# An encoder layer on one core: its attention stage with three engines in a hand-set order

## The chip, the cores and the metric

The kernel runs on one core of one Trainium2 chip. The metric is the device time of one execution, in microseconds (us); the times of three executions of the kernel before are given below. All rows come from one profiled execution. The engines are TensorE (PE, the matrix products; PEld is its weight loading), DVE (VectorE), ACT (ScalarE), POOL (GpSimd) and SP, whose queue issues the DMAs.

## The reference, cut to what matters

One layer with three branches: latent attention with 8 heads over 1024 positions, a short convolution, and cross-attention to 256 memory rows, each with a gate, mixed and projected. All in float32. The change concerns this part:

```
def blocked_bidirectional_attention(q, k, v):      # q, k: 8 heads of 96; v: 8 heads of 64
    def one_block(q_blk):                          # 128 query rows
        s = jnp.einsum('bqhd,bkhd->bhqk', q_blk, k).astype(jnp.float32) * scale
        p = jax.nn.softmax(s, axis=-1).astype(v.dtype)
        return jnp.einsum('bhqk,bkhd->bqhd', p, v)
...
o_attn = blocked_bidirectional_attention(q, k, v) * jax.nn.silu(g_attn)
...
r_attn, r_conv, r_mem = split_cols(jax.nn.sigmoid(r + b_gate), (D_MODEL, D_MODEL, D_MODEL))
y = r_attn * (o_attn @ w_br_attn) + r_conv * (o_conv @ w_br_conv) + r_mem * (o_mem @ w_br_mem)
return x + y @ w_out
```

## The kernel before, in words

A float32 product is made of three products of rounded parts: a value is split into a high half (a rounded copy) and a low half (value minus high half), and high by high, high by low and low by high are added in PSUM. The helper `split` does this with two instructions, the first at L74 (POOL) or L76 (ACT), the second at L80.

The attention stage is the function `mla`. It runs over 64 blocks i of 128 query rows (8 heads, 8 blocks each); two blocks make a pair u. For a block, `sm(i)` makes the scores (six products, L931, into one of two PSUM buffers `s`), the negated row maximum on DVE (L933), the exponential with its row sum on ACT (L936), the reciprocal of the sum (L937), and then turns the block: a float32 cannot be turned by the DMA, so DVE copies its two 16-bit planes into `pl` (`planes`, L85) and two DMA transposes on the SP queue bring them to `plt` (L86). `t(i)` puts the words together again with two ACT copies into `pw` (`words`, L90), then makes the high half `pth` on POOL (L74) and the low half `ptl` on DVE (L80). `pv(u)` needs the halves of both blocks: two small products that spread the reciprocals (L960), eight products with `pth` (L962), eight with `ptl` (L964). It ends with a copy `otmp` on ACT (L971), two additions and scalings on DVE (L972, L973) and, for every second head, a gate and a split on POOL and two stores.

Into this stage the generator `dense` weaves the projection of x that the mixing gates need ("filler products" here, L519, L521 and L523 into `mm`): `pull(n)` takes n of them. 48 belong to one weight tile (an item), whose split on POOL is one pair of instructions of 1024 columns; each 24 are taken out of PSUM by ACT (L613). After the last block come the filler products that are left, then the branch products (L705, L707, L709) with the tiles `oc`, `om` and `oa`.

TensorE's instructions run in the order in which the program writes them (`manual_schedule` from the memory attention on). The order of DVE, ACT, POOL and SP is set by a planner with a cost estimate. Each engine works off its own list in turn, and waits where an operand is not there. In iteration i the program writes: `sm(i)`, 3/8 of the filler products of the iteration, `pv((i-7)/2)` at every second i, `t(i-3)`, the other filler products; 96 filler products are kept for behind the loop.

Of the kernel before, what the change touches and what calls it, by code (L numbers as in the profile page):

```python
# [9 lines left out]
F32 = mybir.dt.float32  # L10
F32R = mybir.dt.float32r
# [3 lines left out]
ALU = mybir.AluOpType  # L15
# [3 lines left out]
P = 128  # L19
S = 1024  # L20
D = 1024
TB = S // P
# [8 lines left out]
NB = 256  # L31
# [30 lines left out]

class K:
# [161 lines left out]
    def phase1(self, sr):  # L225
        tc, nc, a, d = self.tc, self.nc, self.a, self.d
        v, gp = nc.vector, nc.gpsimd
        with ExitStack() as st:
            wk = self.pool(st, "wk0")
# [181 lines left out]
            raws = [load_w(0)]  # L411
# [13 lines left out]
            for t in range(2, TB):  # L425
# [17 lines left out]
                if t >= 3 and up:  # L443
                    src, h_, l_, k = up.pop(0)
                    n = src.shape[-1]
# [7 lines left out]
            ps = self.ps = self.psum(st, "ps00")  # L453
# [1 line left out]
            self.items[0].update(eng="AP")  # L455
            self.gen = self.dense(self.items)
            next(self.gen)
            self.pulled = 0
            self.mm = lambda hf: ps.tile([P, 512], F32, name="fm", bufs=3)
            wd = self.pool(st, "wk1")  # L460
            self.pl = {n: wd.tile([P, 2, H, P], U16, name="pl" + n) for n in "kq"}
# [16 lines left out]
    def dense(self, items):  # L478

        nc = self.nc  # L480
        raws, ws = {}, {}

        def load(i):
            if i < len(items) and i not in raws:
                raws[i] = items[i].get("raw") or self.wp.tile([P, 1024], F32, name="wraw", bufs=2)
                nc.sync.dma_start(raws[i], items[i]["src"])

        def split(i):
            if i < len(items):
                dst = items[i].get("dst")  # L490
                if dst is None:
                    dst = [self.wp.tile([P, 1024], F32R, name=n, bufs=2) for n in ("whi", "wlo")]
                load(i)
                self.split(raws[i], dst[0], dst[1], *items[i].get("eng", "P"))
                ws[i] = dst

        load(0)
        split(0)
        yield
        load(1)  # L500
        i = -1
        while i + 1 < len(items):
            i += 1
            split(i + 1)
            load(i + 2)
            wh, wl = ws.pop(i)
            if "body" in items[i]:
                yield from items[i]["body"](wh, wl)

    def feat(self, fin):  # L510

# [397 lines left out]
    def mla(self, st, sh):  # L909
        tc, nc, a, d = self.tc, self.nc, self.a, self.d  # L910
        v, ps = nc.vector, self.ps
        nj = NB // P
        NBLK = S // NB
        self.o = {}
        wk_s = st.enter_context(ExitStack())
        wk = self.pool(wk_s, "wk5", side="right")
        HD, load = self.HD, self.load_head
        PL, PT, MX, cur = {}, {}, {}, {}

        def sm(i):  # L920
            h, tb = divmod(i, TB)
            k = HD[h][0]
            if i % nj == 0:
                self.load_q(i // nj + 2)
            q = self.QB[i // nj]
            ts = slice(i % nj * P, (i % nj + 1) * P)
            s = ps.tile([P, S], F32, name="s", bufs=2)
            for qi, ki, s_, e_ in ((0, 0, True, False), (0, 1, False, False), (1, 0, False, True)):
                for hf in range(2):
                    c = slice(hf * 512, hf * 512 + 512)  # L930
                    nc.tensor.matmul(s[:, c], q[:, qi, ts], k[:, ki, c], start=s_, stop=e_)  # L931
            mx = MX[i] = wk.tile([P, 4], F32, name="mx", bufs=10)
            v.reduce_max(out=mx[:, 1:2], in_=s, axis=AX.X, negate=True)  # L933
            p = wk.tile([P, S], F32, name="p", bufs=2)

            nc.scalar.activation(out=p, in_=s, func=AF.Exp, bias=mx[:, 1:2], accum_out=mx[:, 2:3])  # L936
            v.reciprocal(mx[:, 3:4], mx[:, 2:3])  # L937
            PL[i] = wk.tile([P, 2, TB, P], U16, name="plt", bufs=3)
            self.planes(p, wk.tile([P, 2, S], U16, name="pl", bufs=2), PL[i])

        def t(i):
            u, j = divmod(i, nj)
            js = slice(j * P, (j + 1) * P)
            if j == 0:
                PT[u] = [wk.tile([P, TB, NB], F32R, name="pt" + x, bufs=2) for x in "hl"]
            p = wk.tile([P, TB, P], F32, name="pw", bufs=2)
            self.words(p, PL.pop(i))
            self.split(p, PT[u][0][:, :, js], PT[u][1][:, :, js], "P", "V")

        def pv(u):  # L950
            h, blk = divmod(u, NBLK)
            bs = slice(blk * NB, (blk + 1) * NB)
            vv = HD[h][1]
            pth, ptl = PT.pop(u)

            pb = ps.tile([P, 2, NB], F32, name="po", bufs=2)
            po, rb = pb[:, 0], pb[:, 1]
            for j in range(nj):
                r = MX.pop(u * nj + j)[:, 3:4]
                nc.tensor.transpose(rb[:, j * P:(j + 1) * P], r.broadcast_to([P, P]), self.ident)  # L960
            for kb in range(TB):
                nc.tensor.matmul(po, vv[:, kb, :], pth[:, kb, :], start=kb == 0, stop=False)  # L962
            for kb in range(TB):
                nc.tensor.matmul(po, vv[:, kb, :], ptl[:, kb, :], start=False, stop=kb == TB - 1)  # L964
            pr, od = divmod(h, 2)
            if od == 0 and blk == 0:
                cur["o"] = wk.tile([P, S], F32, name="o", bufs=1)
            o = cur["o"]
            a0, b0 = (0, 64) if od == 0 else (64, 0)
            tmp = wk.tile([P, NB], F32, name="otmp")  # L970
            nc.scalar.copy(tmp[a0:a0 + 64, :], po[b0:b0 + 64, :])  # L971
            v.tensor_tensor(out=o[a0:a0 + 64, bs], in0=po[a0:a0 + 64, :], in1=tmp[a0:a0 + 64, :], op=ALU.add)  # L972
            v.tensor_tensor(out=o[a0:a0 + 64, bs], in0=rb[a0:a0 + 64, :], in1=o[a0:a0 + 64, bs], op=ALU.mult)  # L973
            if od == 1:
                gp = nc.gpsimd
                oh = wk.tile([P, NB], F32R, name="oah")
                ol = wk.tile([P, NB], F32R, name="oal")
                ga = wk.tile([P, NB], F32, name="ga")
                nc.sync.dma_start(ga, d["ga"][:, pr, bs])
                gp.tensor_tensor(out=o[:, bs], in0=o[:, bs], in1=ga, op=ALU.mult)  # L980
                self.split(o[:, bs], oh, ol)
                nc.sync.dma_start(d["oah"][:, pr, bs], oh.bitcast(F32))
                nc.sync.dma_start(d["oal"][:, pr, bs], ol.bitcast(F32))

        N = H * TB
        r_end = 1248 + 24 * 48
        rest = 96
        for i in range(N + 7):
            if i % TB == TB - 4 and 0 < i // TB < H:
                load(i // TB + 1)  # L990
            n = (r_end - rest - self.pulled) // (N + 7 - i)
            if i < N:
                sm(i)
                self.pull(n * 3 // 8)
            if i == 0:
                with tc.issue_after(self.turned):
                    load(1)
            if i >= 7 and (i - 7) % 2 == 0:
                pv((i - 7) // 2)
            if 0 <= i - 3 < N:  # L1000
                t(i - 3)
            self.pull(n - n * 3 // 8 if i < N else n)
        wk_s.close()
        self.alloc_o(self.pool(self.st, "oc", side="right"), "oc")
        step(self.load_o("oc"))
        self.ahead(2)
        self.pull_to(r_end)
        self.s_kvq.close()
        sh.close()
        self.open_out()  # L1010
# [134 lines left out]
```

## Time and profile before

| | us |
|---|---|
| median of three executions | 1223.88 |
| lowest, highest | 1223.3, 1226.05 |
| the profiled execution | 1220.76 |
| its span, first to last instruction | 1219.0 |
| busy in the span: TensorE, weight loading | 1146.2, 961.0 |
| busy: DVE, ACT, POOL | 709.7, 546.4, 501.9 |
| mean granted clock of TensorE | 0.975 |
| first to last score maximum of the attention stage | 591.1 to 949.4 |

The span is read by stretches, since the stages have different limits. Busy time of TensorE counts a product that runs at half clock as twice the time, so it does not say what is left to gain; the granted clock beside it does (1.00 is 2.4 GHz, 0.50 is 1.2 GHz). A row of the timeline gives start, duration, engine and line of an instruction, and in brackets how long the engine was idle before it and what ended that.

### The profile page before, as it was taken

The numbers are of one execution on the slowest core, as the hardware profiler recorded it, in microseconds if no ns is written. First come the engines' busy times: TensorE is split into PE (matmuls) and PEld (weight loads), VectorE is DVE, ScalarE is ACT, GpSimd is POOL, SyncE is SP. The second block draws the span as 40 slices with busy tenths as digits, with TensorE's granted clock in tenths as the row PEclk, the third lists the DMA queues.
The fourth block names the chain that finished last, engine by engine and source line by source line (L and its number), as shares of the span: only waits on it lengthen the run. The fifth ranks groups of instructions, "written<-read, shape, count | busy, mean of one in ns | idle before, by whom it ended". The sixth has DMA issues, their size and how long they took to land.

```text
span 1219.0 us, 15240 instructions
## 1 busy us (share of the span) xinstructions
PE 1146.2 (94%) x5458; PEld 961.0 (79%) x5458; DVE 709.7 (58%) x1084; ACT 546.4 (45%) x821; POOL 501.9 (41%) x382
## 2 busy tenths in 40 slices
PE   8999998999999999899988979889798999999998
PEld 7998786788888887777766768677687878888887
DVE  6997785253335345553478887878888503655221
ACT  6445766311112035554487676757767522323100
POOL 4456455332325633345334543433554533323200
PEclk8999998999999999999999899998999999999999
DMA  8428999823324243548697896887876589545341
GB/s 304 149 78 203 226 252 233 234 72 104 104 89 136 88 108 100 127 134 223 179 198 179 172 237 168 190 189 162 204 185 147 166 310 387 152 147 171 123 138 52
DMA packets 283821, 207.75 MB, mean 170 GB/s; under 512 B 201440, under 2 KB 253280, under 8 KB 282976
## 3 DMA queue, kind: packets, MB, share of 16 engines
q1 hardware_dynamic: 283744, 206.76, 62.7%
q8 instruction: 43, 0.70, 0.3%
q14 instruction: 34, 0.28, 0.1%
HBM read 108.14 MB, written 50.33 MB: 130 GB/s over the span
## 4 chain that ended last, share of the span: by engine, by line
PE 45%; ACT 14%; DMA 14%; DVE 13%; issue 9%; POOL 4%; SPq 1%; ACTq 0%; DVEq 0%; POOLq 0%
DMA plt<-pl 9%; ACT pw L90 7%; PE mm L519 6%; PE mm L523 6%; PE mm L521 6%; DVE pl L85 5%; PE mm L707 4%; PE mm L705 4%; PE mm L709 4%; ACT p L936 3%; DVE ptl L80 3%; PE mm L109 3%; PE mm L110 3%; PE mm L111 3%; PE pq L293 2%
## 5 line engine op out<-in xcount | busy, mean ns | idle before, releaser
L519 PE MATMUL mm<-hh,whi 128*128 128x512 f32 x672 | 268.9, 400 | 3.4 <-DVE sg L596 2.5
L523 PE MATMUL mm<-hh,wlo 128*128 128x512 f32 x672 | 267.1, 399 | 1.2 <-POOL wlo L80 1.2
L521 PE MATMUL mm<-hl,whi 128*128 128x512 f32 x672 | 267.9, 399 | 0.0
L90 ACT COPY pw<-plt 128x1024 uint16<-128x1024 uint16 (+1 forms) x160 | 201.3, 1300 | 133.7 <-DMA plt<-pl 85.4
L74 POOL TENSOR_SCALAR whi<-wraw 128x1024 fp32r<-128x1024 f32 x59 | 70.5, 1195 | 226.3 <-PE mm L521 78.0
L519 PEld LDWEIGHTS mm<-hh,whi 128*128 128x128 f32 x672 | 130.3, 194 | 31.7 <-DVE sg L596 3.4
L80 POOL TENSOR_TENSOR wlo<-wraw,whi 128x1024 fp32r<-128x1024 f32 x60 | 152.1, 2535 | 5.4 <-ACT whi L76 1.6
L523 PEld LDWEIGHTS mm<-hh,wlo 128*128 128x128 f32 x672 | 130.2, 194 | 29.3 <-POOL wlo L80 1.6
L521 PEld LDWEIGHTS mm<-hl,whi 128*128 128x128 f32 x672 | 130.1, 194 | 27.1
L931 PE MATMUL s<-k,q 96*128 96x512 f32 x384 | 107.4, 417 | 41.3 <-ACT p L936 40.6
L74 POOL TENSOR_SCALAR pth<-pw 128x1024 fp32r<-128x1024 f32 x64 | 82.9, 1299 | 134.8 <-ACT pw L90 115.1
L85 DVE COPY pl<-p 128x1024 uint16<-128x1024 uint16 x144 | 128.8, 936 | 7.8 <-POOL p L830 6.0
L931 PEld LDWEIGHTS s<-k,q 96*128 96x128 f32 x384 | 73.6, 197 | 66.7 <-ACT p L936 50.2
L80 DVE TENSOR_TENSOR ptl<-pw,pth 128x1024 fp32r<-128x1024 f32 x64 | 88.3, 1381 | 5.9 <-POOL pth L74 5.5
L933 DVE TENSOR_REDUCE mx<-s 128x1 f32<-128x1024 f32 x64 | 77.1, 1215 | 6.0 <-PE s L931 5.4
L936 ACT ACTIVATE p<-s,mx 128x1024 f32<-128x1024 f32 x64 | 71.0, 1111 | 12.4 <-DVE mx L933 9.7
L682 ACT ACTIVATE sg<-sg 128x1024 f32<-128x1024 f32 x24 | 25.4, 1062 | 85.9 <-DMA sg<-d_r 81.3
L391 ACT COPY pw<-plt 96x512 uint16<-96x512 uint16 x64 | 43.8, 772 | 27.3 <-DMA plt<-plq 18.6
L613 ACT ACTIVATE sg<-mm,small 128x512 f32<-128x512 f32 x48 | 32.9, 687 | 42.0 <-PE mm L523 37.0
L937 DVE RECIPROCAL mx<-mx 128x1 f32<-128x1 f32 x64 | 10.3, 161 | 60.8 <-ACT p L936 60.6
L712 DVE TENSOR_TENSOR acc<-mm,sg 128x512 f32<-128x512 f32 x16 | 10.8, 688 | 57.0 <-PE mm L709 43.6
L76 ACT CAST whi<-wraw 128x1024 fp32r<-128x1024 f32 x9 | 9.5, 1052 | 68.4 <-PE mm L521 66.8
(322 smaller groups left out, 2359.1 us busy)
## 6 DMA issues: line engine op xcount, KB each, us to landing
wraw<-in_w_feat SPq DMA_DIRECT2D x48, 512.0 KB, 4.3
d_r<-sg SPq DMA_DIRECT2D x24, 512.0 KB, 3.1
sg<-d_r SPq DMA_DIRECT2D x24, 512.0 KB, 3.8
d_k<-qkt SPq DMA_DIRECT2D x32, 192.0 KB, 3.1
d_q<-qkt SPq DMA_DIRECT2D x32, 192.0 KB, 3.1
q<-d_q SPq DMA_DIRECT2D x32, 192.0 KB, 3.3
k<-d_k SPq DMA_DIRECT2D x8, 768.0 KB, 7.3
wraw<-in_w_br SPq DMA_DIRECT2D x12, 512.0 KB, 4.4
```

What stands on the lines that cost most here:

```text
L74: nc.gpsimd.tensor_scalar(out=hi, in0=raw, scalar1=1.0, scalar2=1.0, op0=ALU.mult, op1=ALU.mult)
L80: e.tensor_tensor(out=lo, in0=raw, in1=hi.bitcast(F32), op=ALU.subtract)
L85: self.nc.vector.tensor_copy(pl[:, x], _halves(src, x))
L90: self.nc.scalar.copy(_halves(out, x), plt[:, x])
L519: mm(o, w1, self.hh[:, k, c], start=k == 0, stop=False)
L521: mm(o, w1, self.hl[:, k, c], start=False, stop=False)
L523: mm(o, w2, self.hh[:, k, c], start=False, stop=k == KT - 1)
L705: mm(o, w1, rh[:, k, c], start=k == 0, stop=False)
L707: mm(o, w1, rl[:, k, c], start=False, stop=False)
L931: nc.tensor.matmul(s[:, c], q[:, qi, ts], k[:, ki, c], start=s_, stop=e_)
L933: v.reduce_max(out=mx[:, 1:2], in_=s, axis=AX.X, negate=True)
L936: nc.scalar.activation(out=p, in_=s, func=AF.Exp, bias=mx[:, 1:2], accum_out=mx[:, 2:3])
```

## The change

In `mla`, DVE, ACT and POOL now follow the order in which the program writes the stage, as TensorE did. `sm`, `t` and `pv` are cut into smaller functions and written in a new order. In step i: `exps(i)` (maximum, exponential), half of the filler products, `low(i-4)`, `turn(i)` (planes, transposes, reciprocal), `words(i-2)` (word copies and high half), `pv((i-5)/2)` at odd i, the other filler products, `scores(i+1)`, and at even i `fin((i-6)/2)` (otmp, the two additions, the gate part). There is one buffer `p` instead of two and three `pw` instead of two; the loop has 69 steps instead of 71 iterations, and 72 filler products are kept for behind it instead of 96. In `dense` a weight split is done in quarters of 256 columns, between the filler products of the item before. The loop of filler products, and everything before and behind the stage, stay as they are. Line numbers behind `dense` move: the maximum is L948, the exponential L951, the reciprocal L957, the high half L969, the low half L973, the scores L943, pv L984 and L987, otmp L1003, the additions L1004 and L1005, the evacuation of filler products L620.

```diff
-        def split(i):
+        def split(i, part=0, parts=1):
...
+                c = slice(part * 1024 // parts, (part + 1) * 1024 // parts)
+                self.split(raws[i][:, c], *(t[:, c] for t in ws[i]), *items[i].get("eng", "P"))
...
+            for n, _ in enumerate(items[i]["body"](wh, wl)):
+                if parts > 1 and n % 8 == 2 and n // 8 < parts:
+                    split(i + 1, n // 8, parts)
+                    if n // 8 == parts - 1:
+                        load(i + 2)
+                yield
...
+        self.parts = 4
+        man.enter_context(tc.manual_schedule(engines={E.DVE, E.Activation, E.Pool}))
...
+        def exps(i):
+            s = SC.pop(i)
+            mx = MX[i] = wk.tile([P, 4], F32, name="mx", bufs=12)
             v.reduce_max(out=mx[:, 1:2], in_=s, axis=AX.X, negate=True)
-            p = wk.tile([P, S], F32, name="p", bufs=2)
+            p = PL[i] = wk.tile([P, S], F32, name="p", bufs=1)
 
             nc.scalar.activation(out=p, in_=s, func=AF.Exp, bias=mx[:, 1:2], accum_out=mx[:, 2:3])
...
+        def turn(i):
+            p = PL[i]
             PL[i] = wk.tile([P, 2, TB, P], U16, name="plt", bufs=3)
             self.planes(p, wk.tile([P, 2, S], U16, name="pl", bufs=2), PL[i])
...
+            v.reciprocal(MX[i][:, 3:4], MX[i][:, 2:3])
...
+        def words(i):
+            p = PW[i] = wk.tile([P, TB, P], F32, name="pw", bufs=3)
             self.words(p, PL.pop(i))
-            self.split(p, PT[u][0][:, :, js], PT[u][1][:, :, js], "P", "V")
+            nc.gpsimd.tensor_scalar(out=parts(i)[0], in0=p, scalar1=1.0, scalar2=1.0, op0=ALU.mult, op1=ALU.mult)
+
+        def low(i):
+            hi, lo = parts(i)
+            v.tensor_tensor(out=lo, in0=PW.pop(i), in1=hi.bitcast(F32), op=ALU.subtract)
...
-        rest = 96
-        for i in range(N + 7):
+        rest = 72
+        LAST = N + 4
+        scores(0)
+        for i in range(LAST + 1):
+            j = i + 1
...
-            n = (r_end - rest - self.pulled) // (N + 7 - i)
+            n = (r_end - rest - self.pulled) // (LAST + 1 - i)
             if i < N:
-                sm(i)
-                self.pull(n * 3 // 8)
+                exps(i)
...
-            if i >= 7 and (i - 7) % 2 == 0:
-                pv((i - 7) // 2)
-            if 0 <= i - 3 < N:
-                t(i - 3)
-            self.pull(n - n * 3 // 8 if i < N else n)
+            self.pull(n // 2)
+            if 0 <= i - 4 < N:
+                low(i - 4)
+            if i < N:
+                turn(i)
+            if 0 <= i - 2 < N:
+                words(i - 2)
+            if i >= 5 and i % 2:
+                pv((i - 5) // 2)
+            self.pull(n - n // 2)
+            if j < N:
+                scores(j)
+            if i >= 6 and i % 2 == 0:
+                fin((i - 6) // 2)
```

How the rows of an engine's program moved, at one place in the middle of the stage; equal numbers behind a name are the same buffer use.

DVE over two blocks, before (`mx<-s` is the maximum, `ptl` the low half, `pl` the planes, `o` the two additions):

```order
L933 TENSOR_REDUCE mx_6064<-s_6057 128x1
L973 TENSOR_TENSOR o_5305<-po_6006,o_5305 64x256
L933 TENSOR_REDUCE mx_6097<-s_6090 128x1
L937 RECIPROCAL mx_6064<-mx_6064 128x1
L85 COPY pl_6070<-p_6066 128x1024 x2
L80 TENSOR_TENSOR ptl_6136<-pw_6137,pth_6135 128x8x128
L937 RECIPROCAL mx_6097<-mx_6097 128x1
L85 COPY pl_6103<-p_6099 128x1024 x2
L80 TENSOR_TENSOR ptl_6136<-pw_6181,pth_6135 128x8x128
L972 TENSOR_TENSOR o_6130<-po_6111,otmp_6131 64x256
L933 TENSOR_REDUCE mx_6160<-s_6153 128x1
```

DVE over an odd and an even step, after:

```order
L948 TENSOR_REDUCE mx_5947<-s_5929 128x1
L973 TENSOR_TENSOR ptl_5807<-pw_5857,pth_5806 128x8x128
L85 COPY pl_5962<-p_5949 128x1024 x2
L957 RECIPROCAL mx_5947<-mx_5947 128x1
L948 TENSOR_REDUCE mx_6014<-s_6003 128x1
L973 TENSOR_TENSOR ptl_5918<-pw_5914,pth_5917 128x8x128
L85 COPY pl_6025<-p_6016 128x1024 x2
L957 RECIPROCAL mx_6014<-mx_6014 128x1
L1004 TENSOR_TENSOR o_5303<-po_5972,otmp_6054 64x256
L1005 TENSOR_TENSOR o_5303<-po_5972,o_5303 64x256
L948 TENSOR_REDUCE mx_6065<-s_6047 128x1
```

The two maxima that stood next to each other now stand one in each step, each followed by a low half, and the additions stand together ahead of the odd step's maximum.

ACT at the same place, before (`p,mx` is the exponential, `pw` the word copies, `sg` the evacuation of filler products):

```order
L936 ACTIVATE p_6066,mx_6064<-s_6057,mx_6064 128x1024
L90 COPY pw_6181<-plt_5997 128x1024 x2
L936 ACTIVATE p_6099,mx_6097<-s_6090,mx_6097 128x1024
L971 COPY otmp_6131<-po_6111 64x256
L613 ACTIVATE sg_6048<-mm_6050,small_73 128x512
L90 COPY pw_6239<-plt_6069 128x1024 x2
```

ACT, after:

```order
L951 ACTIVATE p_5949,mx_5947<-s_5929,mx_5947 128x1024
L90 COPY pw_5968<-plt_5850 128x1024 x2
L951 ACTIVATE p_6016,mx_6014<-s_6003,mx_6014 128x1024
L90 COPY pw_6031<-plt_5907 128x1024 x2
L620 ACTIVATE sg_6045<-mm_5926,small_73 128x512
L1003 COPY otmp_6054<-po_5972 64x256
```

The copy otmp now stands behind the word copies of the even step, and every exponential is followed by two word copies.

TensorE from pv to the next scores, before:

```order
L962 MATMUL po_6111<-pth_5932,v_5522 128x256 x8
L964 MATMUL po_6111<-ptl_5933,v_5522 128x256 x8
L523 MATMUL mm_6050<-hh_89,wlo_5651 128x512
L519 MATMUL mm_6050<-hh_89,whi_5650 128x512
L521 MATMUL mm_6050<-hl_90,whi_5650 128x512
```

TensorE in the odd step whose DVE rows stand above, after:

```order
L987 MATMUL po_5972<-pth_5806,v_5027 128x256 x8
L987 MATMUL po_5972<-ptl_5807,v_5027 128x256 x8
L528 MATMUL mm_5926<-hl_90,whi_5700 128x512
L530 MATMUL mm_5926<-hh_89,wlo_5701 128x512
L526 MATMUL mm_5926<-hh_89,whi_5700 128x512
```

TensorE's own sequence is nearly the same (three more filler products and the scores of the next block follow); what differs is that `ptl_5807` is written by DVE in this very step.

## Rows read from the trace of the kernel before

**Rows 1.** Busy time by stretches: us, busy of each engine (instructions), clock, DMA, GB/s.

```profile
615.10:949.40 334.30, 293.74 (x1436) 241.69 (x1435) 272.39 (x345) 237.38 (x284) 150.33 (x119) 0.94 0.80 184
949.40:997.50 48.10, 47.18 (x234) 39.62 (x233) 12.63 (x20) 17.07 (x23) 22.39 (x22) 1.00 0.74 243
```

**Rows 2.** One line, the score maximum: duration ns min/median/max, first and last start.

```profile
L933 DVE TENSOR_REDUCE mx<-s x64: 1204/1216/1226, 591.1 to 949.4; 128x1 f32<-128x1024 f32 x64
```

**Rows 3.** Timeline of DVE: start us, duration us, what; sixth maximum and low half.

```profile
615.08 1.21 DVE L933 TENSOR_REDUCE mx<-s 128x1 f32<-128x1024 f32 x1
616.22 1.21 DVE L80 TENSOR_TENSOR ptl<-pw,pth 128x1024 fp32r<-128x1024 f32 x1
```

**Rows 4.** Waits from 615.1 to 949.4: total us, times, longest us.

```profile
PE s L931 <- ACT p L936: 40.6, 21, 3.9
```

**Rows 5.** Timeline of TensorE: low products, two filler products, scores.

```profile
845.00 1.12 PE L964 MATMUL po<-ptl,v 128*128 128x256 f32 x8
845.96 0.40 PE L519 MATMUL mm<-hh,whi 128*128 128x512 f32 x1
846.19 0.40 PE L521 MATMUL mm<-hl,whi 128*128 128x512 f32 x1
...
847.57 1.55 PE L931 MATMUL s<-k,q 96*128 96x512 f32 x6
```

**Rows 6.** Timeline of ACT: exponential, two word copies; the last otmp.

```profile
845.80 1.12 ACT L936 ACTIVATE p<-s,mx 128x1024 f32<-128x1024 f32 x1
...
846.91 2.58 ACT L90 COPY pw<-plt 128x1024 uint16<-128x1024 uint16 x2
...
969.51 0.36 ACT L971 COPY otmp<-po 64x256 f32<-64x256 f32 x1 [1.90 <-PE po L964]
```

**Rows 7.** Timeline of DVE: an addition and a maximum; the last two additions.

```profile
712.74 0.43 DVE L973 TENSOR_TENSOR o<-po,o 64x256 f32<-64x256 f32 x1
713.20 1.22 DVE L933 TENSOR_REDUCE mx<-s 128x1 f32<-128x1024 f32 x1
...
969.91 0.43 DVE L972 TENSOR_TENSOR o<-po,otmp 64x256 f32<-64x256 f32 x1 [5.01 <-ACT otmp L971]
970.37 0.43 DVE L973 TENSOR_TENSOR o<-po,o 64x256 f32<-64x256 f32 x1
```

**Rows 8.** Groups from 615.1 to 949.4: busy us, mean ns, idle before.

```profile
L85 DVE COPY pl<-p 128x1024 uint16<-128x1024 uint16 x115 | 103.2, 939 | 0.0
L80 DVE TENSOR_TENSOR ptl<-pw,pth 128x1024 fp32r<-128x1024 f32 x59 | 81.7, 1385 | 3.5 <-POOL pth L74 3.2
L613 ACT ACTIVATE sg<-mm,small 128x512 f32<-128x512 f32 x24 | 16.5, 686 | 0.3
```

**Rows 9.** The low half's line alone, columns as in rows 2.

```profile
L80 DVE TENSOR_TENSOR ptl<-pw,pth x64: 1204/1218/3399, 605.3 to 962.7; 128x1024 fp32r<-128x1024 f32 x64
```

**Rows 10.** Timeline of TensorE: scores behind a wait, its length in brackets.

```profile
670.31 2.26 PE L931 MATMUL s<-k,q 96*128 96x512 f32 x6 [3.54 <-ACT p L936]
787.68 2.93 PE L931 MATMUL s<-k,q 96*128 96x512 f32 x6 [2.96 <-ACT p L936]
812.58 1.65 PE L931 MATMUL s<-k,q 96*128 96x512 f32 x6 [2.67 <-ACT p L936]
```

**Rows 11.** Busy time by stretches around these waits; the clock is third from the end.

```profile
665.00:675.00 10.00, 6.46 (x23) 4.80 (x22) 8.41 (x13) 7.92 (x10) 3.13 (x2) 0.83 0.96 246
785.00:792.00 7.00, 4.32 (x10) 3.46 (x11) 6.76 (x9) 5.98 (x9) 4.76 (x5) 0.66 1.03 299
810.00:817.00 7.00, 4.42 (x19) 3.66 (x20) 3.51 (x8) 5.20 (x8) 2.46 (x3) 1.00 0.97 255
```

**Rows 12.** DMA issues with median us to landing; the end of the stage.

```profile
plt<-pl SPq DMA_TRANSPOSE x122, 2.9
...
976.26 0.40 SPq L1020 DMA_DIRECT2D och<-d_och x1
...
997.32 0.39 PE L705 MATMUL mm<-och,whi 128*128 128x512 f32 x1
```

More of the change, by code (lines that the diff above doesn't have):

```diff
@@ L457, in phase1 @@
             next(self.gen)
-            self.pulled = 0
+            self.pulled, self.parts = 0, 1
             self.mm = lambda hf: ps.tile([P, 512], F32, name="fm", bufs=3)
@@ L486, in load @@
                 nc.sync.dma_start(raws[i], items[i]["src"])
-        def split(i):
+        def split(i, part=0, parts=1):
             if i < len(items):
[L490 to L495, printed above, removed]
+                if part == 0:
+                    ws[i] = items[i].get("dst") or [self.wp.tile([P, 1024], F32R, name=n, bufs=2) for n in ("whi", "wlo")]
+                    load(i)
+                c = slice(part * 1024 // parts, (part + 1) * 1024 // parts)
+                self.split(raws[i][:, c], *(t[:, c] for t in ws[i]), *items[i].get("eng", "P"))
         load(0)
@@ L503, in dense @@
             i += 1
-            split(i + 1)
-            load(i + 2)
             wh, wl = ws.pop(i)
-            if "body" in items[i]:
-                yield from items[i]["body"](wh, wl)
+            if self.parts == 1 or "body" not in items[i]:
+                split(i + 1)
+                load(i + 2)
+            if "body" not in items[i]:
+                continue
+            parts = self.parts
+            for n, _ in enumerate(items[i]["body"](wh, wl)):
+                if parts > 1 and n % 8 == 2 and n // 8 < parts:
+                    split(i + 1, n // 8, parts)
+                    if n // 8 == parts - 1:
+                        load(i + 2)
+                yield
     def feat(self, fin):
@@ L917, in mla, with scores @@
         HD, load = self.HD, self.load_head
-        PL, PT, MX, cur = {}, {}, {}, {}
-        def sm(i):
+        SC, PL, PW, PT, MX, GA, PO, cur = {}, {}, {}, {}, {}, {}, {}, {}
+        E = mybir.EngineType
+        man = st.enter_context(ExitStack())
+        self.parts = 4
+        man.enter_context(tc.manual_schedule(engines={E.DVE, E.Activation, E.Pool}))
+        def scores(i):
             h, tb = divmod(i, TB)
@@ L926, in sm @@
             ts = slice(i % nj * P, (i % nj + 1) * P)
-            s = ps.tile([P, S], F32, name="s", bufs=2)
+            s = SC[i] = ps.tile([P, S], F32, name="s", bufs=2)
             for qi, ki, s_, e_ in ((0, 0, True, False), (0, 1, False, False), (1, 0, False, True)):
@@ L931, in sm, with parts @@
                     nc.tensor.matmul(s[:, c], q[:, qi, ts], k[:, ki, c], start=s_, stop=e_)
-            mx = MX[i] = wk.tile([P, 4], F32, name="mx", bufs=10)
+        def exps(i):
+            s = SC.pop(i)
+            mx = MX[i] = wk.tile([P, 4], F32, name="mx", bufs=12)
             v.reduce_max(out=mx[:, 1:2], in_=s, axis=AX.X, negate=True)
-            p = wk.tile([P, S], F32, name="p", bufs=2)
+            p = PL[i] = wk.tile([P, S], F32, name="p", bufs=1)
             nc.scalar.activation(out=p, in_=s, func=AF.Exp, bias=mx[:, 1:2], accum_out=mx[:, 2:3])
-            v.reciprocal(mx[:, 3:4], mx[:, 2:3])
+        def turn(i):
+            p = PL[i]
             PL[i] = wk.tile([P, 2, TB, P], U16, name="plt", bufs=3)
             self.planes(p, wk.tile([P, 2, S], U16, name="pl", bufs=2), PL[i])
-        def t(i):
+            v.reciprocal(MX[i][:, 3:4], MX[i][:, 2:3])
+        def parts(i):
             u, j = divmod(i, nj)
+            if u not in PT:
+                PT[u] = [wk.tile([P, TB, NB], F32R, name="pt" + x, bufs=2) for x in "hl"]
             js = slice(j * P, (j + 1) * P)
-            if j == 0:
-                PT[u] = [wk.tile([P, TB, NB], F32R, name="pt" + x, bufs=2) for x in "hl"]
-            p = wk.tile([P, TB, P], F32, name="pw", bufs=2)
+            return [t[:, :, js] for t in PT[u]]
+        def words(i):
+            p = PW[i] = wk.tile([P, TB, P], F32, name="pw", bufs=3)
             self.words(p, PL.pop(i))
-            self.split(p, PT[u][0][:, :, js], PT[u][1][:, :, js], "P", "V")
+            nc.gpsimd.tensor_scalar(out=parts(i)[0], in0=p, scalar1=1.0, scalar2=1.0, op0=ALU.mult, op1=ALU.mult)
+        def low(i):
+            hi, lo = parts(i)
+            v.tensor_tensor(out=lo, in0=PW.pop(i), in1=hi.bitcast(F32), op=ALU.subtract)
         def pv(u):
             h, blk = divmod(u, NBLK)
-            bs = slice(blk * NB, (blk + 1) * NB)
             vv = HD[h][1]
             pth, ptl = PT.pop(u)
-            pb = ps.tile([P, 2, NB], F32, name="po", bufs=2)
+            pb = PO[u] = ps.tile([P, 2, NB], F32, name="po", bufs=2)
             po, rb = pb[:, 0], pb[:, 1]
@@ L960, in pv, with fin @@
                 nc.tensor.transpose(rb[:, j * P:(j + 1) * P], r.broadcast_to([P, P]), self.ident)
[L961 to L964, printed above, removed]
+            for t, s_, e_ in ((pth, True, False), (ptl, False, True)):
+                for kb in range(TB):
+                    nc.tensor.matmul(po, vv[:, kb, :], t[:, kb, :], start=s_ and kb == 0, stop=e_ and kb == TB - 1)
+            if h % 2:
+                GA[u] = wk.tile([P, NB], F32, name="ga")
+                nc.sync.dma_start(GA[u], d["ga"][:, h // 2, blk * NB:(blk + 1) * NB])
+        def fin(u):
+            h, blk = divmod(u, NBLK)
+            bs = slice(blk * NB, (blk + 1) * NB)
+            pb = PO.pop(u)
+            po, rb = pb[:, 0], pb[:, 1]
             pr, od = divmod(h, 2)
@@ L977, in pv @@
                 ol = wk.tile([P, NB], F32R, name="oal")
-                ga = wk.tile([P, NB], F32, name="ga")
-                nc.sync.dma_start(ga, d["ga"][:, pr, bs])
-                gp.tensor_tensor(out=o[:, bs], in0=o[:, bs], in1=ga, op=ALU.mult)
+                gp.tensor_tensor(out=o[:, bs], in0=o[:, bs], in1=GA.pop(u), op=ALU.mult)
                 self.split(o[:, bs], oh, ol)
@@ L997, in mla @@
                     load(1)
-            if i >= 7 and (i - 7) % 2 == 0:
-                pv((i - 7) // 2)
-            if 0 <= i - 3 < N:
-                t(i - 3)
-            self.pull(n - n * 3 // 8 if i < N else n)
+            self.pull(n // 2)
[12 more added lines that the diff above has]
+                fin((i - 6) // 2)
+        man.close()
+        self.parts = 1
         wk_s.close()
```

## The prediction

> **What bounds the kernel now.** The table by stretches comes first. From the first score maximum (L933) at 591.1 us to the last at 949.4 the attention stage takes 358 us of the 1219 us span; from the sixth maximum (615.08) on, 58 blocks of 128 rows take 334.3 us, 5.76 us a block or 11.53 us for two [rows 1 to 3]. No engine fills that stretch: TensorE 293.7, DVE 272.4, ACT 237.4, POOL 150.3 [rows 1]. The view of waits says what happens in the rest: TensorE stands before the score products (L931) for 40.6 us in 21 waits, each ended by an exponential that frees a score buffer [rows 4]. The granted clock says what these waits cost on top: 0.94 in that stretch, against 1.00 behind it [rows 1]. So the stage is a chain of engines that wait for each other, and the question is not whether each engine has less to do but how long the new ring of waits is.
>
> **The change, part by part.** Work is neither added nor removed, except that a weight split becomes four smaller ones. What changes is order, and how far one step lies behind another.
>
> *The ring.* A round is two steps, odd then even. In program order TensorE's step i is: half of the filler products, at odd i pv of blocks i-5 and i-4, the other half, scores of block i+1. DVE's is: maximum i, low half i-4, two planes, reciprocal, at even i the two additions of fin. ACT's: exponential i, two word copies, at even i the copy otmp. Two links close a ring. (1) In an odd step pv reads the low half that DVE makes in that very step; before, t ran at iteration i-3 and pv at i-7, so that the low half had three iterations' time. Behind pv on TensorE stand the scores of the next block. (2) In an even step DVE must finish fin before the next maximum, and fin waits for otmp, which on ACT stands behind the exponential of this step and both word copies; before, the planner put a maximum between the two additions, and otmp where ACT was free.
>
> Odd half, from the start of a maximum: 1.14 us to the start of the low half [rows 3]; the low half 1.385 on average [rows 8]; 0.04 to hand over (as from otmp's end at 969.87 to the addition at 969.91 [rows 6, 7]); pv's eight low products 845.00 to 845.96, 0.96 us; then 5.83 filler products (six in 24 of the 29 odd steps before a score product, five in the other five) at 0.23, 1.35 us; the six score products 1.55 [rows 5]; 0.04. Together 6.46 us.
>
> Even half: maximum 1.22 [rows 2] and 0.04; from the exponential's start to the first word copy 1.11, two word copies 2.58 [rows 6], 0.03; otmp 0.36 and 0.04; first addition to second 0.46 [rows 7], second to the next maximum 0.46 [rows 7]. Together 6.30 us. In 13 of the 29 even steps an L613 evacuation of the filler products also stands between exponential and otmp: 0.69 us each [rows 8], of which 0.65 taken, 13 x 0.65 = 8.5 us.
>
> Steps 5 to 63 are 29 rounds: 29 x 12.76 + 8.5 = 378.5 us against 334.3, **44.2 us more**.
>
> *Start.* Steps 0 to 4 have neither pv nor fin: a maximum 1.22, an exponential some 1.2 [rows 2, 6], two planes at up to 0.94 each [rows 8], so 3.8 to 4.4 us on DVE beside TensorE's 11 filler and six score products, 3.9; I take 4.0 us a step, 20 us against the 24.0 from 591.1 to 615.08 [rows 2, 3]: **4.0 less**.
>
> *End.* When the last maximum starts, TensorE in the changed kernel waits 2.4 us for the low half and has eight low products, 133 filler products and two pv of 2.2 us left before the next phase: 2.4 + 1.0 + 30.8 + 4.4 = 38.6 us at full clock. Before, the same point to the first product of the next phase (997.32) is 47.9 us [rows 2, 12]. The next phase needs the oc tiles, which load only when the last fin has released the pool: at 976.26, 6.8 us behind the last otmp; from that otmp (969.51) to the next phase there are 27.8 us before [rows 6, 12]. Now 89 filler products lie behind the last pv, 20.6 us. Between nothing and those 7 us can show as a new wait; I take 3. **6.3 less**.
>
> *Quarter splits.* The last quarter of an item is issued after 26 of the 48 filler products of the item before, 22 products or two steps ahead of its use; POOL is busy for 150 of 334 us [rows 1]. I cost them at nothing; the cover is those two steps, without it TensorE would wait for a quarter of a split (a whole one is two POOL instructions, so about a microsecond) once an item, 15 times. Between the pairs stand POOL's high halves, needed two steps later: a step to spare. *Transposes*: each is issued two steps before its word copies; in rounds of 13 us that is over 13 us for a landing of 2.9 [rows 12]: hidden.
>
> *The low half and POOL.* The low half has a floor of 1.204 us, a median of 1.218 and a maximum of 3.399; the maximum over scores, next to it on the same engine, stays within 1.204 to 1.226 [rows 2, 9]. The Trainium skill's page SBUF — State Buffer (Who interferes with whom) says that a DVE instruction with two SBUF inputs blocks against a GpSimd instruction that reads SBUF, while a reduction does not; these rows agree. I take the mean, 1.385; at the median the ring is 4.8 us shorter over 29 rounds. By the rule every low half that meets one of POOL's casts would wait up to a whole cast, 29 us or so more in all; the traced mean speaks for less.
>
> *The clock.* TensorE's work in a round is 21.7 filler products 5.0, twelve score products 2.8, pv 2.1, 9.9 us. So it waits 2.8 us in a plain round and 3.5 in one with an L613 copy in the even step, before pv's low products, in one piece; the profile counts some 0.2 less, the tail of the last product. In the trace all five waits of 2.96 us and more end at the lower of the two levels, 1.2 GHz instead of 2.4, or reach it within the next six products (2.96 at 787.68: the scores take 2.93 us; 3.54 at 670.31: 2.26); one of 2.67 (812.58: 1.65) does not [rows 10, 11]. So I let the 13 longer waits fall and not the others. Behind the wait stands just the piece of TensorE's work that is on the ring. The price of a fall: granted 0.66 over 7 us is 2.4 us lost, 0.83 over 10 us is 1.7 [rows 11]; I take 2.3, as the stretch begins where the ring needs TensorE. 13 x 2.3 = **30 us**; ends 0 and 29 x 2.4 = 70.
>
> Sum against the profiled execution, 1220.8 us: + 44.2 - 4.0 - 6.3 + 30 = **1285 us**. The median of the runs shown lies 3 us above that execution; I leave that in the range.
>
> **The rivals.**
> *The clock holds.* If no wait of the ring lowers the clock: 1285 - 30 = 1255, down to 1242 with undisturbed low halves, no wait for oc and evacuations that cost half. For it: the wait of 2.67 us passed at full clock [rows 10]. Against: the wait comes every round, and is longer in 13 of them.
> *The clock falls in every round.* 1255 + 29 x 2.3 = 1322, or 1325 at 2.4. For it: the wait comes in every round, and the plain round's 2.6 us lies next to the 2.67 that passed once. Against: that it did pass. The Trainium skill's page TensorE: Matmul & The Clock Gate (HAM oscillation — how this bites in real kernels) tells of a loop that waited in each turn and began each turn cold, which is this rival. By that rule the time is the 1322; the trace agrees for its longer waits only.
> *The engines' own work sets the pace, and the kernel is faster.* If the low half were ready when pv comes and otmp when DVE comes, DVE would be the bound with 272.4 / 58 = 4.70 us a block, TensorE with 4.97 (9.94 / 2): 58 x (5.76 - 5.0) = 44 us less, start and end 10 us less, about 1167. It decides from the point where pv's low half is a step old; its place is the two links. For it: the planner's order shows 40.6 us of waits that evenly spaced exponentials take away. Against: both links stand in the rows of the changed program, in turn, with nothing of the same engine to pass them.
> *The change doesn't do what it says* is shut out by the same rows: the three engines do stand in the fixed order. That gains and losses cancel to within 0.2%, about what a measurement of this kernel can tell from no change, needs the ring 1.5 us shorter than its floors.
>
> **How the numbers follow.** Forecast (falls in about half of the rounds, 1262 to 1310) 0.45; clock holds (1242 to 1262) 0.24; clock falls in every round, or nearly (1310 to 1335) 0.18; a longer ring still, by POOL or transposes 0.04; engines' own work 0.07; no difference 0.02. The range 1242 to 1328 leaves out the last three and the upper part of the third, about 0.2. Faster 0.07, same 0.02, slower 0.91.
>
> **What would show it.** In the changed profile: maxima (L948) 6.3 to 7 us apart from the sixth on; TensorE's largest waits before the low products of pv, ended by DVE's low half; DVE waiting before the maximum of even steps for the scores and before fin for otmp, some 30 times each; the waits for the exponential before the scores gone. The clock in the stage tells 1255 from 1285 and 1322. I am wrong if two blocks take under 12 us, or if TensorE still waits for exponentials.

## The result, and the profile after

The changed kernel takes 1297.89 us (median of four executions, 1292.12 to 1302.17) against 1224.97 for the kernel before: 1.0589 times as long, 95% interval 1.0541 to 1.0638. The profiled execution took 1302.17 us, its span is 1300.2, the mean granted clock 0.949.

The stretches that answer to [rows 1 to 3] come first: start to sixth maximum, the 58 blocks from the sixth to the last, to the first branch product, and the rest (us, then busy us of PE, PEld, DVE, ACT and POOL with their instructions, clock, DMA share, GB/s).

```profile
591.70:611.90 20.20, 20.20 (x93) 16.58 (x92) 14.66 (x23) 13.28 (x17) 6.80 (x8) 1.00 0.77 167
611.90:1029.60 417.70, 334.83 (x1503) 279.14 (x1501) 251.44 (x349) 239.69 (x289) 165.40 (x200) 0.89 0.63 152
1029.60:1071.00 41.40, 37.53 (x177) 31.58 (x178) 13.02 (x15) 15.69 (x18) 27.92 (x33) 0.96 0.55 173
1071.00:1300.20 229.20, 222.45 (x1009) 184.22 (x1007) 90.02 (x118) 37.67 (x44) 54.08 (x30) 0.99 0.51 178
```

The 58 blocks took 334.3 us before and take 417.7 now, 7.20 us a block instead of 5.76, and the clock in them is 0.89 instead of 0.94. All of the loss is there. The waits in that stretch (engine and line that wait, what they wait for, total us, times, longest) answer to [rows 4]:

```profile
DVE mx L948 <- PE s L943: 104.5, 29, 5.3
...
PE po L987 <- DVE ptl L973: 82.2, 29, 3.7
DVE o L1004 <- ACT otmp L1003: 45.2, 26, 2.1
```

TensorE no longer waits for an exponential before the scores (40.6 us in 21 waits before); it waits before pv's low products, once in each of the 29 rounds. DVE waits for the scores 29 times and for otmp 26 times. One round in the timelines of the three engines (start us, duration us, engine, line; in brackets the idle time before and what ended it), an even step and the odd step behind it. DVE:

```profile
634.05 1.22 DVE L948 TENSOR_REDUCE mx<-s 128x1 f32<-128x1024 f32 x1 [3.30 <-PE s L943]
...
639.46 0.42 DVE L1004 TENSOR_TENSOR o<-po,otmp 64x256 f32<-64x256 f32 x1 [1.49 <-ACT otmp L1003]
639.91 0.42 DVE L1005 TENSOR_TENSOR o<-po,o 64x256 f32<-64x256 f32 x1
640.25 1.21 DVE L948 TENSOR_REDUCE mx<-s 128x1 f32<-128x1024 f32 x1
641.38 1.21 DVE L973 TENSOR_TENSOR ptl<-pw,pth 128x1024 fp32r<-128x1024 f32 x1
...
648.00 1.23 DVE L948 TENSOR_REDUCE mx<-s 128x1 f32<-128x1024 f32 x1 [3.84 <-PE s L943]
```

ACT in the even step:

```profile
635.37 1.12 ACT L951 ACTIVATE p<-s,mx 128x1024 f32<-128x1024 f32 x1 [3.54 <-DVE mx L948]
...
636.47 2.56 ACT L90 COPY pw<-plt 128x1024 uint16<-128x1024 uint16 x2
639.06 0.37 ACT L1003 COPY otmp<-po 64x256 f32<-64x256 f32 x1
```

TensorE in the odd step:

```profile
638.82 1.20 PE L987 MATMUL po<-pth,v 128*128 128x256 f32 x8
642.65 1.76 PE L987 MATMUL po<-ptl,v 128*128 128x256 f32 x8 [2.63 <-DVE ptl L973]
...
646.34 1.62 PE L943 MATMUL s<-k,q 96*128 96x512 f32 x6
```

The ring can be walked in these rows: maximum 634.05, exponential 635.37, word copies 636.47, otmp 639.06, additions 639.46 and 639.91, maximum 640.25, low half 641.38, low products 642.65, scores until 647.96, maximum 648.00. No step of it has slack. The even half is 6.20 us. The odd half is 7.75, because the low products and the filler products behind them run at the lower clock: the eight low products take 1.76 us instead of the 1.12 of [rows 5], and the granted clock from 642.65 to 646.34 is 0.56.

### The profile page after: what moved, and what is told of

The parts are those of the page before. It is cut to its first block, busy times and chain, and to the rows that moved or that the text cites. A ratio compares the mean times of both kernels' runs of the same rounds, so it can differ in the third digit from the quotient of the medians.

```text
span 1300.2 us, 15302 instructions
## 1 busy us (share of the span) xinstructions
PE 1177.9 (91%) x5458; PEld 989.6 (76%) x5458; DVE 691.6 (53%) x1084; ACT 545.6 (42%) x821; POOL 519.3 (40%) x478
## 4 chain that ended last, share of the span: by engine, by line
PE 51%; DVE 13%; issue 11%; ACT 10%; DMA 7%; POOL 7%; SPq 1%; POOLq 0%; ACTq 0%; DVEq 0%
PE mm L530 7%; PE mm L526 7%; PE mm L528 6%; ACT pw L90 5%; DVE mx L948 4%; PE po L987 4%; PE mm L714 3%; PE mm L716 3%; PE mm L712 3%; PE s L943 3%; DVE ptl L973 3%; PE mm L109 2%; PE mm L111 2%; PE mm L110 2%; PE pq L293 2%
## 5 line engine op out<-in xcount | busy, mean ns | idle before, releaser
L530 PE MATMUL mm<-hh,wlo 128*128 128x512 f32 x672 | 271.6, 406 | 0.8 <-POOL wlo L80 0.8
L90 ACT COPY pw<-plt 128x1024 uint16<-128x1024 uint16 (+1 forms) x160 | 196.7, 1296 | 36.9 <-DMA plt<-pl 35.2
L969 POOL TENSOR_SCALAR pth<-pw 128x1024 fp32r<-128x1024 f32 x64 | 67.0, 1047 | 255.4 <-ACT pw L90 255.2
L74 POOL TENSOR_SCALAR whi<-wraw 128x256 fp32r<-128x256 f32 (+1 forms) x107 | 85.3, 797 | 209.1 <-PE pm L761 76.4
L80 POOL TENSOR_TENSOR wlo<-wraw,whi 128x256 fp32r<-128x256 f32 (+1 forms) x108 | 162.4, 1503 | 11.0 <-PE tr L318 1.5
L951 ACT ACTIVATE p<-s,mx 128x1024 f32<-128x1024 f32 x64 | 71.4, 1116 | 183.0 <-DVE mx L948 183.0
L987 PE MATMUL po<-ptl,v 128*128 128x256 f32 x256 | 55.5, 381 | 86.7 <-DVE ptl L973 86.7
L948 DVE TENSOR_REDUCE mx<-s 128x1 f32<-128x1024 f32 x64 | 78.0, 1218 | 105.0 <-PE s L943 104.5
L85 DVE COPY pl<-p 128x1024 uint16<-128x1024 uint16 x144 | 108.6, 796 | 21.1 <-ACT p L951 14.6
L987 PEld LDWEIGHTS po<-ptl,v 128*128 128x128 f32 x256 | 46.9, 270 | 93.2 <-DVE ptl L973 93.2
L943 PE MATMUL s<-k,q 96*128 96x512 f32 x384 | 104.1, 408 | 0.8 <-ACT sg L620 0.8
L943 PEld LDWEIGHTS s<-k,q 96*128 96x128 f32 x384 | 77.5, 202 | 19.9 <-ACT sg L620 1.2
L973 DVE TENSOR_TENSOR ptl<-pw,pth 128x1024 fp32r<-128x1024 f32 x64 | 81.8, 1279 | 0.5
L620 ACT ACTIVATE sg<-mm,small 128x512 f32<-128x512 f32 x48 | 32.8, 685 | 56.4 <-PE mm L530 40.7
L1004 DVE TENSOR_TENSOR o<-po,otmp 64x256 f32<-64x256 f32 x32 | 13.5, 422 | 64.5 <-ACT otmp L1003 59.3
```

What stands on the lines that cost most here:

```text
L85: self.nc.vector.tensor_copy(pl[:, x], _halves(src, x))
L530: mm(o, w2, self.hh[:, k, c], start=False, stop=k == KT - 1)
L973: v.tensor_tensor(out=lo, in0=PW.pop(i), in1=hi.bitcast(F32), op=ALU.subtract)
L987: nc.tensor.matmul(po, vv[:, kb, :], t[:, kb, :], start=s_ and kb == 0, stop=e_ and kb == TB - 1)
```

## The experiments

Each kernel ran beside the kernel before, with its ratio taken on the same chip. The runs were taken on more than one chip, where the kernel before had medians of 1219.82 to 1224.97 us, so differences of medians between two of them are good to some 5 us. The halves are means of the distances between the starts of the maxima from the sixth to the last (odd: from an odd step's maximum to the next; even: the other). In "pv a step later" pv and fin trade steps, so its halves don't answer to the others'.

| kernel | median us | ratio, 95% interval | odd half us | even half us | sixth to last maximum us |
|---|---|---|---|---|---|
| the changed kernel | 1297.89 | 1.0589, 1.0541 to 1.0638 | 7.87 | 6.53 | 417.7 |
| low half a block sooner | 1190.87 | 0.9752, 0.9726 to 0.9779 | 4.24 | 6.63 | 315.2 |
| otmp first | 1231.09 | 1.0081, 1.0054 to 1.0107 | 7.43 | 4.76 | 353.4 |
| both | 1175.75 | 0.9626, 0.9593 to 0.9659 | 4.86 | 5.37 | 296.6 |
| TensorE kept busy | 1263.41 | 1.0337, 1.0307 to 1.0367 | 6.56 | 6.53 | 379.9 |
| whole splits | 1307.11 | 1.0703, 1.0675 to 1.0731 | 8.10 | 6.54 | 424.6 |
| pv a step later, otmp first | 1171.36 | 0.9605, 0.9569 to 0.9642 | 5.45 | 4.65 | 292.9 |
| both, whole splits | 1193.41 | 0.9774, 0.9747 to 0.9801 | 4.96 | 6.11 | 321.2 |
| both, words first | 1196.68 | 0.9793, 0.9758 to 0.9828 | 4.89 | 5.96 | 314.4 |

**Link 1 cut: the low half one block behind, not two.**

```diff
-            if 0 <= i - 4 < N:
-                low(i - 4)
+            if 0 <= i - 3 < N:
+                low(i - 3)
```

> Only change to the changed kernel: step i makes the low half of block i-3 instead of i-4, so that pv in an odd step reads low halves that are a step old (link 1 of the ring cut; fin still waits for otmp behind the word copies). Ring theory: the odd half falls from 7.9 us to DVE's own 4.2 to 4.5 (1.14 + 1.28 + exponential wait + two planes), the even half stays at 6.2 to 6.9, TensorE's wait before pv's low products goes and with it the clock falls; a round of about 10.9 instead of 14.4, 29 x 3.5 = 101 us less: about 1197, 1185 to 1210. Rival, that quarter splits and POOL's fixed order hold the stage up: the low half then waits for the high half, and the time stays within 15 us of 1298.

1190.87 us; odd half 4.24, even half 6.63, clock 0.989 over the span. One number moved, and the loss became a gain: TensorE's wait for the low half is 3.6 us in 16 waits from 616 to 905 us (82.2 in 29 in the changed kernel's stretch). What DVE waits for in that stretch is the other link, and the high half, which is now only a step old:

```profile
DVE ptl L973 <- POOL pth L969: 25.1, 27, 1.7
DVE o L1004 <- ACT otmp L1003: 16.4, 21, 1.7
```

**Link 2 cut: otmp ahead of the exponential, fin behind the low half.**

```diff
+            if i >= 6 and i % 2 == 0:
+                otmp((i - 6) // 2)
             if i < N:
                 exps(i)
...
                 low(i - 4)
+            if i >= 6 and i % 2 == 0:
+                fin((i - 6) // 2)
...
-            if i >= 6 and i % 2 == 0:
-                fin((i - 6) // 2)
```

> Only change to the changed kernel: in even steps ACT makes otmp ahead of the exponential, and DVE makes fin's two additions right behind the low half, ahead of the planes (link 2 cut, link 1 stays). Ring theory: the even half falls from 6.5 to about 4.9 (maximum, low half, two additions, two planes), the odd half stays at least 6.4. TensorE's wait before pv's low products shrinks from some 2.9 to 1.5 us, so the clock holds: round 11.4, 29 x 3.0 = 87 us less, about 1211. If the clock still falls in each round, 12.8 and 1251. Rival as in the first run: within 15 us of 1298.

1231.09 us, between the two numbers given: the even half fell to 4.76, and the odd half stayed on 6.4 to 7.2 us in 19 of 29 rounds, with 8.6 to 8.7 in ten. So the clock still fell, in a third of the rounds. Another part of the miss from 1211 is the low half of the odd steps: 1.73 us on average here, 1.28 in the changed kernel, 13 us over 29 rounds.

**Both links cut.**

> Both edits above, so no link of the ring is left. Ring theory: the engines' own work sets the pace, DVE some 9.2 us a round, TensorE 9.94: 29 x 10 = 290 us for the stretch that took 417.7, about 1170, up to 1190 if high halves or transposes come late (the low half of block i-3 needs a high half made one step before). It would beat both kernels. Rival, that the fixed order itself costs (no planner to fill gaps): slower than 1225.

1175.75 us. From 616 to 905 us DVE has no wait for otmp, and TensorE waits for the low half for 3.2 us in 8 waits; what is left on DVE is the wait for the high half, made only a step before, 29.0 us in 39. TensorE sets the pace: it is busy for 283.8 of 289 us at full clock (PE is the first of the five).

```profile
616.00:905.00 289.00, 283.77 (x1458) 238.10 (x1457) 255.34 (x341) 233.84 (x281) 189.60 (x196) 1.00 0.97 211
```

Against the kernel before, the sixth to the last maximum is 38 us shorter, with some 60 more TensorE products in it by the records (1497 against 1436); with whole splits, below, it is still 13 us shorter. So a fixed order need not cost anything; the distances in this one did. The other parts of the change (one buffer `p`, three `pw`, 72 kept products) were not varied.

**The clock's share: TensorE kept busy while it waits.**

```diff
+            for _ in range(16):
+                nc.tensor.matmul(rb, vv[:, 0, :], pth[:, 0, :], start=True, stop=True)
             for j in range(nj):
                 r = MX.pop(u * nj + j)[:, 3:4]
```

> The changed kernel with 16 products of 256 columns added before each pv, written to a place that pv's first small products overwrite; they add about 1.9 us of work for TensorE inside its wait of some 2.9 us, so the wait is about 1 us. Theory, that the odd halves are longer than 6.4 us only through the clock that falls after the wait: the clock stays at 1.00, odd halves 6.4 to 6.6, 29 x 1.4 = 40 us less in spite of more work, about 1258. Rival, that odd halves are long for another reason: 1298 within 8, or above by what the added products cost.

1263.41 us. With 16 more products a round the kernel is 34 us faster. A round here, DVE's maxima and the low products:

```profile
631.74 1.23 DVE L948 TENSOR_REDUCE mx<-s 128x1 f32<-128x1024 f32 x1 [1.75 <-PE s L943]
637.96 1.21 DVE L948 TENSOR_REDUCE mx<-s 128x1 f32<-128x1024 f32 x1
644.15 1.23 DVE L948 TENSOR_REDUCE mx<-s 128x1 f32<-128x1024 f32 x1 [2.29 <-PE s L943]
```

```profile
640.36 1.21 PE L989 MATMUL po<-ptl,v 128*128 128x256 f32 x8 [0.72 <-DVE ptl L973]
```

The odd half from 637.96 is 6.19 us instead of 7.75, the even half the same 6.2. From the low products to the scores it is 640.36 to 642.57, 2.21 us at a granted clock of 1.00, where the round above needs 3.69 at 0.56. The means, 6.56 and 6.53, are the ring at full clock, but for one round in which the clock still fell (8.38 us); what the changed kernel has above it, 417.7 - 379.9 = 37.8 us, is the clock's.

**Whole weight splits in the changed kernel.**

```diff
-        self.parts = 4
+        self.parts = 1
```

> The changed kernel with weight splits undivided again (1024 columns at the start of an item), everything else as changed. The prediction costed the quarters at nothing: a high half is needed two steps after it is made, so a POOL pair of some 3.5 us in one piece fits. Expected 1298 within 6. Rival, that quarters are part of the loss (more POOL instructions beside DVE's low halves): 1285 or less; rival, that quarters protect the ring: above 1306.

1307.11 us: missed by 3 us, on the side of "quarters protect the ring". The groups of the low half from the sixth to the last maximum (busy us, mean ns, idle before), in the changed kernel and then with whole splits, show how:

```profile
L973 DVE TENSOR_TENSOR ptl<-pw,pth 128x1024 fp32r<-128x1024 f32 x58 | 72.4, 1249 | 0.4
```

```profile
L973 DVE TENSOR_TENSOR ptl<-pw,pth 128x1024 fp32r<-128x1024 f32 x58 | 81.3, 1401 | 0.4
```

The high half isn't late, as expected; the low half itself lasts longer, 1.40 against 1.25 us, with a longest of 3.05 against 2.05. One low half a round is on the ring, that of the odd step: 1.38 against 1.28 us, 29 x 0.10 = 3 of the 6.9 us by which the stretch is longer. The rest goes with the clock, which fell in 25 odd halves instead of 22.

**Link 1 cut the other way: pv and fin a step later.**

```diff
-            if i >= 5 and i % 2:
-                pv((i - 5) // 2)
+            if i >= 6 and i % 2 == 0:
+                pv((i - 6) // 2)
...
-        LAST = N + 4
+        LAST = N + 5
```

with otmp and fin as in "otmp first", at odd i for pair (i-7)/2, and the low half at i-4.

> Link 1 cut the other way: the low half stays at block i-4, pv moves one step on (even steps, blocks i-6 and i-5) and fin to the odd step after, with otmp ahead of the exponential as in the run with both edits. There DVE waited 37.9 us in 44 waits for a high half made only one step before; here it is two steps old again. Theory, that pv must only be a step behind the low half, whichever of the two moves: 1165 to 1180, those waits under 5 us. Rival, that the gain came from the earlier low half: 1230 or more.

1171.36 us, the fastest here, 4% below the kernel before; its interval overlaps that of "both", so which of the two is better isn't settled. DVE's waits for the high half from 616 to 905 us are down to 2.3 us in 3, from 29.0 in 39. TensorE is busy for 282.9 of 289 us. The DMA engines' share, 0.63 in the changed kernel, is 0.98, at 211 GB/s; whether they would be the next bound is not shown, since a share of 1.02 went with 411 GB/s elsewhere (the stretch behind 1071.0, below).

```profile
616.00:905.00 289.00, 282.93 (x1462) 239.00 (x1461) 270.20 (x344) 237.14 (x284) 201.19 (x195) 0.99 0.98 211
```

**Whole splits with both links cut.**

> The run with both links cut (1176), with weight splits undivided. There a low half is due one step after its high half, so a POOL pair of 3.5 us ahead of a high half should now show, once an item, 15 times by up to 2.6 us: 1185 to 1210. Rival, that TensorE's pace hides it: 1176 within 4.

1193.41 us, 18 us more than with quarters: the time is as expected, and the POOL pair in one piece does show, but not by the way that was expected. From 616 to 905 us DVE waits for the high half as before, 29.1 us in 39 waits against 29.0 in 39. What got longer is DVE's own work beside POOL's long instruction, the planes above all (two copies, 1.3 us where nothing holds them up). One such place, POOL and then DVE:

```profile
691.38 3.25 POOL L80 TENSOR_TENSOR wlo<-wraw,whi 128x1024 fp32r<-128x1024 f32 x1
692.30 4.34 DVE L85 COPY pl<-p 128x1024 uint16<-128x1024 uint16 x2
```

The planes of the stretch, with quarters and then whole:

```profile
L85 DVE COPY pl<-p 128x1024 uint16<-128x1024 uint16 x116 | 95.0, 859 | 2.3 <-DMA plt<-pl 1.1 <-ACT p L951 0.5 <-issue 0.2
L85 DVE COPY pl<-p 128x1024 uint16<-128x1024 uint16 x117 | 113.6, 1011 | 1.8 <-ACT p L951 1.2
```

Eleven times in the stretch the two copies take 3.0 us or more, each time beside an undivided `wlo`, the low half of a weight. TensorE's waits for the two halves grow with it, 17.3 us against 5.1 from 616 to 905; how much of the 18 us is the planes' and how much a high half that comes late for TensorE was not separated. So the quarters are worth 18 us in the faster kernel, and in the changed kernel 9 by the medians or 14 by the ratios.

**Words ahead of the exponential, with both links cut.**

```diff
+            if 0 <= i - 2 < N:
+                words(i - 2)
             if i >= 6 and i % 2 == 0:
                 otmp((i - 6) // 2)
             if i < N:
                 exps(i)
...
-            if 0 <= i - 2 < N:
-                words(i - 2)
```

> The run with both links cut (1176), with the word copies of block i-2 and then otmp ahead of the exponential of block i, as before the change they often stood. ACT needs 2.6 us for the copies and can begin them when the last exponential ends; at 5.1 us a step they end about when DVE ends the next maximum, so an exponential starts some 0 to 1 us later and DVE's planes with it: 1176 to 1200. Rival, that words behind the exponential is what carries the gain: above 1215.

1196.68 us, 21 more, at the upper end of what was expected. ACT now waits for transposes, 54.9 us in 38 waits from 600 to 1000 us, ahead of the exponential; behind it that wait was hidden. So two parts of the change, the quarters and the words behind the exponential, pay where both links are cut, and the third, the distance of the low half from pv, is where the loss lies, together with the place of otmp.

## Why the prediction was right, point by point

The forecast was 1285 us in 1242 to 1328, slower; 1297.89 lies in the range and in the bracket of the forecast's own case (1262 to 1310). Its terms against the profiled executions (sixth to last maximum is the stretch of [rows 1]):

| term | predicted us | measured us | from |
|---|---|---|---|
| odd half at full clock | 6.46 | 6.56 | TensorE kept busy |
| even half, with its share of evacuations | 6.30 + 8.5 / 29 = 6.59 | 6.53 | the changed kernel |
| the ring against before | + 44.2 | 379.9 - 334.3 = + 45.6 | TensorE kept busy |
| the clock on top | + 30 | 417.7 - 379.9 = + 37.8 | difference of the two |
| start | - 4.0 | 20.2 - 24.0 = - 3.8 | stretches |
| end | - 6.3 | 41.4 - 47.9 = - 6.5 | stretches |
| behind the first branch product | 0 | 229.2 - 221.7 = + 7.5 | stretches |

The measured terms add up to + 80.6 against + 81.4 between the two profiled executions; the forecast's added up to + 64.

*The ring* was right in its mechanism and in its size. That the two links close it is shown, not only argued: each cut took away its own half and left the other one standing, and with both cut the third rival's pace appeared. That rival's figure, 1167 us, was off by 9 us from the 1175.75 of the kernel that fulfils its condition. Inside the odd half two errors nearly cancel: the low half of the odd step took 1.28 us, not the 1.385 of the sum, while low products and filler products took 2.45 us at full clock, not 0.96 + 1.35, and the low half began 1.18 us behind the maximum, not 1.14.

*The clock* was right in kind and wrong in its rule. The step that failed is "I let the 13 longer waits fall and not the others". In the changed kernel 22 of the 29 odd halves are 7.6 us or longer, plain rounds with waits of 2.6 us among them (the round at 642.65). Twelve of the 13 longer waits lie in the stretch; the clock fell behind 8 of them, and behind 14 of the 17 others, so the choice told nothing. The price was over-estimated instead: 37.8 / 22 = 1.7 us, not 2.3. The two errors partly cancelled: the number of falls lies nearer to the rival in which the clock falls in every round, and that the time lies in the bracket of the forecast is in part luck. Nor does the length of a wait tell the rounds apart: behind 3.21 and 3.40 us the eight low products ran at full clock, 1.22 us.

```profile
716.29 1.22 PE L987 MATMUL po<-ptl,v 128*128 128x256 f32 x8 [3.21 <-DVE ptl L973]
...
729.92 1.22 PE L987 MATMUL po<-ptl,v 128*128 128x256 f32 x8 [3.40 <-DVE ptl L973]
```

The loop that the Trainium skill's page TensorE: Matmul & The Clock Gate (HAM oscillation — how this bites in real kernels) describes, which waited in each turn and began each turn cold, came nearer. In this trace it is three rounds in four, 22 of 29.

*The end* was right in sum. The wait for the oc tiles, 3 us in the forecast, came behind the first branch products and not before them, so it stands in the last term; the end lacks it and was 3 us longer than its other terms, 41.4 against 38.6: some 1.7 us for the clock (0.96 over 41.4 us), and two more waits for the low half, 0.49 and 0.60 us, that the sum left out. The rest of the 7.5 us is the clock again: in the 29 us behind 1071.0 TensorE waits 3.5 us for och and ocl, and the granted clock is 0.88 (3.5 us lost); the kernel before has 1.00 in these 29 us, and both have 1.00 behind them.

```profile
1071.00:1100.00 29.00, 25.53 (x96) 19.38 (x95) 4.06 (x6) 2.32 (x3) 6.87 (x4) 0.88 1.02 411
```

*The quarters* were costed at nothing; they gave some 9 us (1307.11 against 1297.89). The forecast's sum didn't carry this, since it took the low half at the 1.385 us of [rows 8], which is also what the odd steps' low half takes with whole splits, 1.38. The Trainium skill's page SBUF — State Buffer (Who interferes with whom) says that a DVE instruction with two SBUF inputs contends with a GpSimd instruction that reads SBUF. The trace agrees: the low half's longest shrinks with POOL's pieces, from 3.05 to 2.05 us, and the maximum's stays at 1.23. The prediction's strict form of it, a whole cast for every low half that meets one, would have made the ring 29 us longer; the odd steps' low half took 1.28 us on average against its floor of 1.20, 2 us over 29 rounds.

*Transposes* were hidden, as said: ACT had no wait for them in the stretch.

## What to carry to other kernels

Before a fixed order is written, write down for each wait across engines how many steps old its operand is; a wait whose operand is made in the same step on another engine joins the two engines' lists, and two such joints make a ring whose length is the sum of its pieces, however idle the engines are. Walk that ring with durations from the trace and compare it with the busiest engine's work per round; here one index (a low half one block behind instead of two) was worth some 100 us (1297.89 to 1190.87). Here a step of distance was enough, and it could be bought on either side of the joint.

## What the runs showed of the hardware that was not expected

The length of the wait before doesn't tell by itself whether the granted clock falls. In "otmp first", waits of 2.16 and 2.17 us stood before pv's low products; behind some the eight products took 1.95 to 2.08 us, behind others 1.21 or 1.22. The granted clock in the 3.85 us from 717.35 is 0.57, in the 2.43 us from 776.37 it is 1.00.

```profile
717.35 2.08 PE L987 MATMUL po<-ptl,v 128*128 128x256 f32 x8 [2.16 <-DVE ptl L973]
...
776.37 1.22 PE L987 MATMUL po<-ptl,v 128*128 128x256 f32 x8 [2.17 <-DVE ptl L973]
...
788.76 1.95 PE L987 MATMUL po<-ptl,v 128*128 128x256 f32 x8 [2.16 <-DVE ptl L973]
...
816.58 1.21 PE L987 MATMUL po<-ptl,v 128*128 128x256 f32 x8 [2.17 <-DVE ptl L973]
```

Of its 13 waits between 2.1 and 2.4 us, ten were followed by an odd half of 8.6 or 8.7 us and three were not; of the 16 waits of 1.3 us or less, none. In the kernel before, a wait of 2.67 us passed [rows 10]. What sets the ones apart that fell was not settled. Products without use, put into the wait, kept the clock up in 28 of 29 rounds and made the kernel 34 us faster, which no sum of work would have said. And DVE's copies of the planes, 1.3 us where nothing holds them up, took 3.0 to 4.4 us beside a POOL instruction of 3.25 us.
